# Slots of the LRU, the order of the last projections, and HGRN scores per head in a hybrid recurrent trunk

## The chip, the cores and the metric

The kernel runs on one core of one Trainium2 chip, in one launch. The metric is the time of one execution in microseconds on the device. A profiled execution gives a page and a trace; its span is the time from the first to the last instruction that the profiler saw. Engines are PE (TensorE; PEld is its weight load), DVE (VectorE), ACT (ScalarE), POOL (GpSimd) and SP, which only starts transfers.

## What is computed

One layer of a trunk with 1024 channels reads a prompt of 1024 tokens and eight single tokens of other sequences with states of their own. RMSNorm, one input projection with 3456 columns, three groups of heads that read the same input, one output projection with a residual, and an MLP of width 4096. Cut to what matters here, for HGRN2 (6 heads, 64 keys, 64 values, chunks of 64 tokens) and for the RG-LRU (256 channels):

```python
# RWKV-7, 6 heads: per token, S = S*diag(w) + (S @ -kk)(kk*a)^T + v k^T;  out = S r
# HGRN2, per head and chunk of 64 tokens, b = cumsum(log f):
dmat = exp(b[t] - b[s]) where s <= t
att[t, s] = sum_k q[t, k] * kin[s, k] * dmat[t, s, k]
o = att @ v + (q * exp(b)) @ S
S = exp(b_last)[:, None] * S + (kin * exp(b_last - b)).T @ v
# RG-LRU: xb, gate = split(pl);  h[t] = a[t] h[t-1] + u[t];  out = h * gelu(gate)
```

Everything is float32. Dense projections are done as three products of rounded halves: each operand is split into a high part (wh, xh) and the rest (wl, xl), and wh·xh, wh·xl and wl·xh are added.

## The kernel before

The prompt is cut into two halves of 512 tokens (the second carries the eight single tokens as well). RWKV and HGRN each have three pairs of heads; one pair fills the 128 partitions, a head on each 64. A step such as h1 is pair 1 of HGRN, r2 pair 2 of RWKV, l0 the first 128 channels of the LRU, w the low-rank columns of RWKV. Names end in the pair and the half: in2944_1_0 is the projection's columns from 2944 (l0's first) in half 1.

**Order on PE.** PE's row is written in program order; the other engines' order is made by a scheduler. The function weave (L106) merges seven recurrent streams and a filler. The streams are the inverses of RWKV (products W and Y, L624), its chains over chunks (ch, L703), its finish (L758), HGRN with the single tokens (L928 to L1115) and the LRU (L1148); two of them are inverses. The filler is projections() (L1334), which yields dense products: the input projection in the order of the table ORDER, then the output projection (out0 to out7) and the first part of the MLP. weave keeps a clock of its own, now; each stream yields a due time (D1 to D42, from a table) or an event to wait for, and whenever no stream is due, a filler row is taken. Where the filler can't go on, the small products of the streams stand in PE's row by themselves.

**Slots.** The outputs of a projection stay in tiles until their recurrence has run. take("hpm") (L398) makes the filler wait until one of eight slots is free. A pair of HGRN takes four (th, q, iv, gs), a tile of the LRU three: xb, gl and gq, the square of gl that the tanh form of GeLU needs. hg_run and lru give them back at their ends.

**Weights.** load_w (L283) loads 512 KB through SP into raw and rounds it to wh on ACT (L291). For names in SOON, DVE subtracts to get wl (L293); for the others ACT writes −wh and a transfer on POOL's queue adds the weights to it (L295, L296). There are two buffers each of wh and wl.

**HGRN's scores.** The exponent of b[t] − b[s] is not bounded as a product of two factors over a whole chunk, so the scores are built on six levels. On level l, blocks of 2·2^l tokens are halved; scaled (L964) makes, with b relative to the block's middle, keys kq for the earlier half and queries rq for the later half, and gram (L984) multiplies them. In gram the eight chunks are eight fp32 matmuls. The lhsT is a chunk of kq on 128 rows (two heads of 64 keys, 64 tokens), the rhs a chunk of rq with 64 columns: 32 later tokens for head 0 and 32 for head 1. That both heads can share the rows, rq is padded: for head 0's columns the rows of head 1 are zero and the other way round. Two such tiles, rqs, are zeroed once and used by turns, and DVE writes the two non-zero quarters in two operations (L981). The result, 128 × 256 in one PSUM bank, is put into att under a mask by one copy_predicated (L992). PSUM tag h has two banks, so the next level can run while the copy of this one is still to come. A level is run six times for three pairs and two halves, 36 in all. An fp32 matmul is recorded as two instructions on PE: a gram of eight is x16 in the profile.

The other names: ho are HGRN's outputs, hoT their transposes, hsq and hso the head norms and sample outputs, oT and gate the finish of RWKV, gs and hs values of roots on POOL (L152), lg the gates of the LRU.

Of the kernel before, what the change touches and what calls it, by code (L numbers as in the profile page):

```python
# [9 lines left out]
F32 = mybir.dt.float32  # L10
F32R = mybir.dt.float32r
I32 = mybir.dt.int32
AF = mybir.ActivationFunctionType
ALU = mybir.AluOpType
# [3 lines left out]
P = 128  # L18
# [7 lines left out]
HT = 512  # L26
HW = HT + NB
QT = 256
NQ = QT // 64
C = 64  # L30
NCK = HT // C
# [9 lines left out]
SOON = tuple(f"in{col}_0" for col in (1152, 1280, 0, 384, 768, 2944, 3200, 1408, 1792, 2176, 2560)) + \  # L41
    ("out0_0", "out1_0") + tuple(f"out{m}_1" for m in range(8)) + tuple(f"w1_{f}" for f in range(4))
PRI = [-100, 0, 0, 300, 300, 300, 100, 300]
ORDER = [[(x[0], int(x[1])) for x in half.split()] for half in ("r0 w0 l0 h0 r1 l1 h1 r2 h2", "w0 r0 h0 r1 h1 r2 h2 l0 l1")]
NFB = FF // (FB * P)

COL_R, COL_K, COL_V, COL_WA, COL_G = 0, 384, 768, 1152, 1280
# [1 line left out]
COL_LX, COL_LG = 2944, 3200  # L49
# [3 lines left out]
def kernel(ctx: ExitStack, tc: tile.TileContext, i, o):  # L53
    nc = tc.nc
    V, S, G, PE = nc.vector, nc.scalar, nc.gpsimd, nc.tensor
    act = S.activation
# [7 lines left out]
    def ps(tag, name):  # L64
        return psum.tile([P, 512], F32, tag=tag, name=name, bufs=PS_BUFS[tag])
# [6 lines left out]
    def mm(out, lhsT, rhs, start=True, stop=True):  # L72
        n, m = rhs.free_size(), lhsT.free_size()
        reshape(lhsT.shape[0], m)
        now[0] += n / 2200 if rhs.dtype == F32R else max(n, 112) / 580 if m > 64 else max(n, 36) / 1000
        PE.matmul(out, lhsT, rhs, start=start, stop=stop)  # L76
# [67 lines left out]
    def bc(ap, shape):  # L144
        return ap.to_broadcast(shape)
# [32 lines left out]
    id64, smask, lmask = cmask[:, 0, :], cmask[:, 1:3, :], cmask[:, 3:9, :]  # L178
# [217 lines left out]
    free = {"pm": RPM, "hpm": HPM}  # L396
# [30 lines left out]
    def take_out(hf, out, pt):  # L427

        if hf == 0:
            V.tensor_tensor(out, pt, rb0, op=ALU.mult)  # L430
        else:
            S.copy(out, pt)
# [518 lines left out]
    def hg_half(j, hf, lf, kin, q, iv, gs):  # L951
# [8 lines left out]

        att = pool.tile([P, 2, NCK // 2, C], F32, tag="att", name=f"att_{n}", bufs=1)
        A4 = [P, 2, NCK // 2, C]

        def scaled(l):  # L964

            hh = 1 << l
            kq = pool.tile([P, HW], F32, tag="kq", name=f"kq{l}_{n}", bufs=2)[:, 0:HT]
            rq = rqs[l % 2]
            pat = "p (m r j) -> p m r j"
            b4 = bf.rearrange(pat, r=2, j=hh)  # L970
            k4 = kq.rearrange(pat, r=2, j=hh)
            nblk = HT // (2 * hh)
            V.tensor_tensor(k4, b4, bc(b4[:, :, 0:1, hh - 1:hh], [P, nblk, 2, hh]), op=ALU.subtract)
            act(k4[:, :, 0, :], k4[:, :, 0, :], AF.Exp, scale=-1.0)
            act(k4[:, :, 1, :], k4[:, :, 1, :], AF.Exp)
            kin4 = kin[:, 0:HT].rearrange(pat, r=2, j=hh)
            q4 = q[:, 0:HT].rearrange(pat, r=2, j=hh)
            G.tensor_tensor(k4[:, :, 0, :], k4[:, :, 0, :], kin4[:, :, 0, :], op=ALU.mult)
            for h in range(2):
                hp = slice(h * 64, h * 64 + 64)  # L980
                V.tensor_tensor(rq[hp, h, :].rearrange("p (m j) -> p m j", j=hh), k4[hp, :, 1, :], q4[hp, :, 1, :], op=ALU.mult)  # L981
            return kq, rq

        def gram(l, kq, rq):  # L984

            hh = 1 << l
            pt = ps("h", f"gram{l}_{n}")[:, 0:4 * C]
            pt4 = pt.rearrange("p (h c t) -> p h c t", h=2, t=C // 2)
            for c in range(NCK):
                op_ = slice((c % 2) * 64, (c % 2) * 64 + 64)  # L990
                mm(pt4[op_, :, c // 2, :], kq[:, c * C:(c + 1) * C], rq[:, :, c * C // 2:(c + 1) * C // 2])
            V.copy_predicated(att.rearrange("p h c (m r j) -> p (h c) m r j", r=2, j=hh)[:, :, :, 1, :],  # L992
                              bc(lmask[:, l, :].rearrange("p (m r j) -> p m r j", r=2, j=hh)[:, None, :, 1, :].bitcast(I32),
                                 [P, NCK, C // (2 * hh), hh]),
                              pt.rearrange("p (x m j) -> p x m j", x=NCK, j=hh))


        vt_ = pool.tile([P, 4, P], F32, tag="vt", name=f"vt_{n}", bufs=1)
# [130 lines left out]
    def lru_proj(t, hf):  # L1129
        if hf == 1:  # L1130
            yield ("LRU", t, 0)
        x = []
        for w in ("xb", "gl", "gq"):
            yield from take("hpm")
            x.append(hp_tile(f"l{w}{t}_{hf}"))
        xb, gl, gq = x
        G.tensor_copy(xb[:, 0:3], lcar[:, t, 0:3])
        yield from in_proj(hf, COL_LX + t * P, lambda pt, c0, n: take_out(hf, xb[:, 3 + c0:3 + c0 + n], pt))

        def evac_g(pt, c0, n):  # L1140
            take_out(hf, gl[:, c0:c0 + n], pt)
            act(gq[:, c0:c0 + n], gl[:, c0:c0 + n], AF.Square)

        yield from in_proj(hf, COL_LG + t * P, evac_g)
        lruin[t, hf] = x
        ev(("lru", t, hf), 1.5)

    def lru(t, hf):  # L1148
        yield ("lru", t, hf)
        xb, gl, gq = lruin[t, hf]  # L1150
        n = HT if hf == 0 else HW
        s0 = hf * HT

        def f(ap):
            return ap[:, 0:n]


        V.tensor_scalar(f(gq), f(gq), 0.044715, 1.0, op0=ALU.mult, op1=ALU.add)
        V.tensor_tensor(f(gq), f(gq), f(gl), op=ALU.mult)
        act(f(gq), f(gq), AF.Tanh, scale=math.sqrt(2.0 / math.pi))  # L1160
        V.scalar_tensor_tensor(f(gl), f(gq), 1.0, f(gl), op0=ALU.add, op1=ALU.mult)

        def cw(j):
            return vec("cw", 2 * j + t)

        xc = hgp.tile([P, HW], F32, tag="xc", name=f"lxc{t}_{hf}", bufs=1)
        V.tensor_scalar(f(xc), xb[:, 3:3 + n], cw(3), vec("cb", t), op0=ALU.mult, op1=ALU.add)
        cv = cst[:, t, 0:24].rearrange("p (b j) -> p b j", j=3)
        for j in range(3):
            V.scalar_tensor_tensor(xc[:, 0:HT], xb[:, j:j + HT], cw(j), xc[:, 0:HT], op0=ALU.mult, op1=ALU.add)  # L1170
            if hf == 1:
                V.scalar_tensor_tensor(xc[:, HT:HW], cv[:, :, j], cw(j), xc[:, HT:HW], op0=ALU.mult, op1=ALU.add)
        if hf == 0:
            V.tensor_copy(lcar[:, t, 0:3], xb[:, HT:HT + 3])
        else:

            so = small.tile([P, 36], F32, tag="lso", name=f"lso{t}", bufs=1)
            V.tensor_copy(so[:, 9:12], xb[:, HT:HT + 3])
            sv = so[:, 12:36].rearrange("p (b j) -> p b j", j=3)
            V.tensor_copy(sv[:, :, 0:2], cv[:, :, 1:3])  # L1180
            V.tensor_copy(sv[:, :, 2], xb[:, 3 + HT:3 + HW])
        rt, it = xb, gq
        yield D39
        for g, (dst, bias) in enumerate(((rt, hba), (it, hbx))):
            for c0, w in (((0, 512),) if hf == 0 else ((0, 260), (260, 260))):
                pt = yield from bank_o(f"lg{t}_{g}_{hf}_{c0}")
                mm(pt[:, 0:w], lruw[:, 2 * g + t, :], xc[:, c0:c0 + w])
                used_o()
                act(dst[:, c0:c0 + w], pt[:, 0:w], AF.Tanh, bias=bias[:, t:t + 1], scale=0.5)
                yield D40  # L1190

        V.scalar_tensor_tensor(f(xc), f(it), 1.0, f(xc), op0=ALU.add, op1=ALU.mult)
        m = gq
        act(f(m), f(rt), AF.Exp, bias=nsp2[:, t:t + 1], scale=nsp2[:, t:t + 1])
        act(f(rt), f(rt), AF.Tanh, bias=sp2[:, t:t + 1], scale=sp2[:, t:t + 1])
        V.scalar_tensor_tensor(f(m), f(m), 1.0, f(rt), op0=ALU.add, op1=ALU.mult)
        V.tensor_scalar(f(rt), f(m), -1.0, 1.0, op0=ALU.mult, op1=ALU.add)

        V.scalar_tensor_tensor(f(m), f(rt), 1.0, f(m), op0=ALU.add, op1=ALU.mult)
        V.tensor_scalar(f(m), f(m), 1e-12, None, op0=ALU.max)  # L1200
        act(f(m), f(m), AF.Sqrt)
        V.scalar_tensor_tensor(f(m), f(m), 0.5, f(xc), op0=ALU.mult, op1=ALU.mult)
        hs = xc
        V.tensor_tensor_scan(hs[:, 0:HT], rt[:, 0:HT], m[:, 0:HT], 0.0 if hf == 0 else lcar[:, t, 3:4], op0=ALU.mult, op1=ALU.add)
        if hf == 1:
            V.tensor_tensor(hs[:, HT:HW], rt[:, HT:HW], cst[:, t, 24:32], op=ALU.mult)
            V.tensor_tensor(hs[:, HT:HW], hs[:, HT:HW], m[:, HT:HW], op=ALU.add)
        V.scalar_tensor_tensor(mix[6 + t][:, s0:s0 + n], f(gl), 0.5, f(hs), op0=ALU.mult, op1=ALU.mult)
        free["hpm"] += 3
        ev(("LRU", t, hf), 14.0)  # L1210
        if hf == 0:
            V.tensor_copy(lcar[:, t, 3:4], hs[:, HT - 1:HT])
            return
        V.tensor_copy(so[:, 0:9], hs[:, HT - 1:HW])
        nc.gpsimd.dma_start(o["lru"][t], so)
# [390 lines left out]
```

## Time and profile before

| what | us |
| --- | --- |
| median of three runs | 1594.58 |
| the three runs | 1597.8, 1592.06, 1594.58 |
| the profiled execution | 1598.09 |
| its span | 1596.3 |
| the scores on PE, 576 records, busy | 24.7 |
| the projection's three products on PE, busy | 222.2, 220.6, 221.7 |
| the square of gl on ACT, six operations, busy | 2.8 |

A row of the profile's groups or of the timeline names line, engine, operation and tile, with shapes as partitions by elements (for a matmul the lhsT as rows by columns, then the output), the number of instructions after x, and times. In the timeline the first number is the start within the span and the second how long it took, both in us; in brackets stands how long the engine had stood idle before it, and what it waited for. In the groups, busy us and mean ns of one come first, then the idle time before. In the waits view the numbers are us in total, how many, and the longest. In the windows view each engine has its busy time in the stretch and the number of its instructions; PEclk is the clock that TensorE was granted, as a share of full speed. Matmuls follow each other in a pipeline, so a row's own length runs into the next; the distance between starts is what a row costs.

### The profile page before, as it was taken

What the parts mean: (1) busy time and instruction counts of PE and PEld (TensorE: products, weight loads), DVE (VectorE), ACT (ScalarE), POOL (GpSimd) and SP (SyncE); (2) the same over time, 40 slices, a digit from 0 to 9 for tenths busy, and PEclk for the clock granted to TensorE, in tenths of its full rate; (3) what the DMA queues carried; (4) which work ended last, traced back from release to release, by engine and by line L of the source; (5) the groups of instructions that cost most, each with busy time, mean ns of one, the idle gap of its engine ahead of it and who ended that gap; (6) DMA issues with size and microseconds to landing.
All of it is one profiled execution on the core that took longest, in us unless ns stands there. A gap on an engine that the chain in (4) does not pass through costs nothing.

```text
span 1596.3 us, 30293 instructions
## 1 busy us (share of the span) xinstructions
PE 1501.6 (94%) x12536; PEld 1323.8 (83%) x12536; DVE 770.7 (48%) x1799; ACT 664.2 (42%) x1435; POOL 382.8 (24%) x531
## 2 busy tenths in 40 slices
PE   8879998998998989888899999999999999999997
PEld 6767776898997888777698989998989998989887
DVE  7778756766466657764465322222222222322224
ACT  4544656546346454454344423233232423233132
POOL 4553224225235245232222010101111010111011
PEclk9999999999899999978899999999999999999999
DMA  4325334334233344204533453535454454544242
GB/s 160 115 68 107 80 76 93 72 81 112 61 82 90 71 103 100 55 29 114 139 110 103 106 92 82 106 80 106 80 106 80 99 100 90 96 88 98 53 94 107
DMA packets 53081, 146.89 MB, mean 92 GB/s; under 512 B 6960, under 2 KB 7248, under 8 KB 52944
## 3 DMA queue, kind: packets, MB, share of 16 engines
q0 software_dynamic: 22976, 65.33, 24.7%
q1 hardware_dynamic: 29824, 79.61, 15.5%
q8 instruction: 98, 1.61, 0.4%
q14 instruction: 39, 0.32, 0.1%
q10 hardware_dynamic: 144, 0.04, 0.0%
HBM read 138.87 MB, written 6.07 MB: 91 GB/s over the span
## 4 chain that ended last, share of the span: by engine, by line
PE 45%; issue 5%; DMA 4%; DVE 3%; ACT 2%; POOL 1%; POOLq 0%; ACTq 0%; DVEq 0%
PE up L76 21%; PE dn L76 20%; PE out L76 2%; DMA raw_out<-in_w_out 1%; DMA wl_out<-in_w_out 1%; DMA wl_w<-in_w 1%; DMA raw_w<-in_w 1%; PE ch L76 1%; ACT wh_out L291 1%; PE in L76 1%; DVE wl_out L293 0%; PE fin L81 0%; DMA w<-in_w 0%; DVE ml L1244 0%; ACT wh_w L291 0%
## 5 line engine op out<-in xcount | busy, mean ns | idle before, releaser
L76 PE MATMUL in<-xl,wh_in 128*128 128x512 f32 (+3 forms) x648 | 222.2, 343 | 1.9 <-DVE xl L385 1.9
L76 PE MATMUL in<-xh,wl_in 128*128 128x512 f32 (+3 forms) x648 | 220.6, 340 | 3.4 <-DMA wl_in<-in_w_in 1.9
L76 PE MATMUL dn<-hh,wl_w 128*128 128x264 f32 (+2 forms) x696 | 222.9, 320 | 0.7 <-DMA wl_w<-in_w 0.6
L76 PE MATMUL dn<-hh,wh_w 128*128 128x264 f32 (+2 forms) x696 | 223.0, 320 | 0.0
L76 PE MATMUL dn<-hl,wh_w 128*128 128x264 f32 (+2 forms) x696 | 222.9, 320 | 0.0
L76 PE MATMUL in<-xh,wh_in 128*128 128x512 f32 (+3 forms) x648 | 221.7, 342 | 0.0
L1494 DVE TENSOR_TENSOR mix<-mix,dn 128x512 f32<-128x512 f32 (+2 forms) x192 | 98.3, 512 | 242.6 <-PE dn L76 242.6
L296 POOL DMA_DIRECT2D wl_w<-in_w x86 | 75.0, 875 | 574.4 <-ACT hh L1424 301.2
L291 ACT ACTIVATE wh_w<-raw_w 128x512 fp32r<-128x512 f32 (+1 forms) x90 | 70.6, 785 | 281.0 <-PE dn L76 228.2
L1423 DVE SCALAR_TENSOR_TENSOR rl<-up,rl 128x512 f32<-128x512 f32 (+2 forms) x96 | 49.5, 516 | 202.2 <-ACT rl L1422 202.2
L76 PE MATMUL up<-nxh,wh_w 128*128 128x264 f32 (+1 forms) x512 | 144.9, 283 | 0.1
L76 PE MATMUL up<-nxl,wh_w 128*128 128x264 f32 (+1 forms) x512 | 144.2, 282 | 0.5 <-POOL nxl L1320 0.5
L76 PE MATMUL up<-nxh,wl_w 128*128 128x264 f32 (+1 forms) x512 | 144.5, 282 | 0.0
L76 PEld LDWEIGHTS dn<-hh,wl_w 128*128 128x128 f32 x696 | 130.9, 188 | 13.6 <-DMA wl_w<-in_w 3.6
L76 PEld LDWEIGHTS dn<-hl,wh_w 128*128 128x128 f32 x696 | 131.0, 188 | 10.1
L76 PEld LDWEIGHTS dn<-hh,wh_w 128*128 128x128 f32 x696 | 131.1, 188 | 9.5
L76 PEld LDWEIGHTS in<-xl,wh_in 128*128 128x128 f32 x648 | 126.5, 195 | 14.6 <-DVE xl L385 4.6
L76 PEld LDWEIGHTS in<-xh,wl_in 128*128 128x128 f32 x648 | 126.3, 195 | 14.1 <-DMA wl_in<-in_w_in 2.4
L76 PEld LDWEIGHTS in<-xh,wh_in 128*128 128x128 f32 x648 | 126.3, 195 | 9.6 <-issue 0.2
L76 PE MATMUL up<-nh,wh_w 128*128 128x512 f32 x256 | 101.6, 397 | 0.0
L76 PE MATMUL up<-nl,wh_w 128*128 128x512 f32 x256 | 101.6, 397 | 0.0
L76 PE MATMUL up<-nh,wl_w 128*128 128x512 f32 x256 | 101.5, 397 | 0.0
(461 smaller groups left out, 3283.6 us busy)
## 6 DMA issues: line engine op xcount, KB each, us to landing
raw_in<-in_w_in SPq DMA_DIRECT2D x53, 512.0 KB, 3.3
wl_in<-in_w_in POOLq DMA_DIRECT2D x43, 512.0 KB, 5.5
raw_w<-in_w SPq DMA_DIRECT2D x32, 512.0 KB, 3.3
raw_w<-in_w SPq DMA_DIRECT2D x64, 256.0 KB, 2.6
wl_w<-in_w POOLq DMA_DIRECT2D x58, 256.0 KB, 4.1
wl_w<-in_w POOLq DMA_DIRECT2D x28, 512.0 KB, 5.5
raw_out<-in_w_out SPq DMA_DIRECT2D x16, 512.0 KB, 3.4
out_y_prompt<-yt SPq DMA_DIRECT2D x16, 256.0 KB, 2.0
```

Source lines behind the costliest of these rows:

```text
L76: PE.matmul(out, lhsT, rhs, start=start, stop=stop)
L291: act(wh[:, ks], raw[:, ks], AF.Copy)
L296: G.dma_start(wl[:, ks], src[:, ks], accum_op=ALU.add)
L1423: V.scalar_tensor_tensor(rl[:, :n], pt[:, :n], 0.0, rl[:, :n], op0=ALU.max, op1=ALU.mult)
L1494: V.tensor_tensor(x2[m][:, c0:c0 + n], x2[m][:, c0:c0 + n], pt[:, :n], op=ALU.add)
```

## The change

There are three edits.

The order of the second half's projections becomes w0 r0 h0 r1 **r2 h1 h2** l0 l1 in place of w0 r0 h0 r1 **h1 r2 h2** l0 l1.

The LRU takes two slots. gq is no longer made when the gate's columns come out of PSUM, in two parts, but in lru itself, in one operation over all columns, into a tile of its own with a single buffer.

HGRN's scores are computed per head. The queries are one tile rql without padding: 256 columns, both heads on their own rows, in two halves used by turns, written by one DVE operation a level; the padded tiles rqs stay for the queries of ho. gram does sixteen matmuls: for each chunk and head one with 64 rows, 64 columns of kq and 32 of rq. Each head writes a bank of its own, so a level takes both banks of tag h, and each head has a masked copy of half the size.

```diff
-ORDER = [... ("r0 w0 l0 h0 r1 l1 h1 r2 h2", "w0 r0 h0 r1 h1 r2 h2 l0 l1")]
+ORDER = [... ("r0 w0 l0 h0 r1 l1 h1 r2 h2", "w0 r0 h0 r1 r2 h1 h2 l0 l1")]
...
+        rql = pool.tile([P, 2, HT // 2], F32, tag="kt", name=f"rql_{n}", bufs=1)
...
-            rq = rqs[l % 2]
+            rq = rql[:, l % 2]
...
+            V.tensor_tensor(rq.rearrange("p (m j) -> p m j", j=hh), k4[:, :, 1, :], q4[:, :, 1, :], op=ALU.mult)
+            return kq, rq
+
+        def gram(l, kq, rq):
+
+            hh = 1 << l
+
+            pts = [ps("h", f"gram{l}_{h}_{n}")[:, 0:2 * C] for h in range(2)]
+            for c in range(NCK):
+                for h, hp in enumerate(brow):
+                    mm(pts[h][(c % 2) * 64:(c % 2) * 64 + 64, c // 2 * (C // 2):(c // 2 + 1) * (C // 2)], kq[hp, c * C:(c + 1) * C], rq[hp, c * C // 2:(c + 1) * C // 2])
             for h in range(2):
-                hp = slice(h * 64, h * 64 + 64)
-                V.tensor_tensor(rq[hp, h, :].rearrange("p (m j) -> p m j", j=hh), k4[hp, :, 1, :], q4[hp, :, 1, :], op=ALU.mult)
-            return kq, rq
-
-        def gram(l, kq, rq):
-
-            hh = 1 << l
-            pt = ps("h", f"gram{l}_{n}")[:, 0:4 * C]
-            pt4 = pt.rearrange("p (h c t) -> p h c t", h=2, t=C // 2)
-            for c in range(NCK):
-                op_ = slice((c % 2) * 64, (c % 2) * 64 + 64)
-                mm(pt4[op_, :, c // 2, :], kq[:, c * C:(c + 1) * C], rq[:, :, c * C // 2:(c + 1) * C // 2])
-            V.copy_predicated(att.rearrange("p h c (m r j) -> p (h c) m r j", r=2, j=hh)[:, :, :, 1, :],
...
+                V.copy_predicated(att[:, h].rearrange("p c (m r j) -> p c m r j", r=2, j=hh)[:, :, :, 1, :],
...
-        for w in ("xb", "gl", "gq"):
+        for w in ("xb", "gl"):
...
-            take_out(hf, gl[:, c0:c0 + n], pt)
-            act(gq[:, c0:c0 + n], gl[:, c0:c0 + n], AF.Square)
...
+        gq = hgp.tile([P, HW], F32, tag="lq", name=f"lq{t}_{hf}", bufs=1)
...
+        act(f(gq), f(gl), AF.Square)
...
-        free["hpm"] += 3
+        free["hpm"] += 2
```

The order of instructions moves with it. First PE, at the place where before the projection of l0 (in3200 is its second half) ends and that of l1 can't start; W, Y and ch are the inverse and the chain of RWKV's pair 2, half 1, gram the scores of h2 in half 1, lg the gates of l0. Before:

```order
L76 MATMUL in3200_1_256_8092<-xh7_3192,wl_in3200_1_7686 128x264
L76 MATMUL gram4_2_1_8186<-rq0_196,kq4_2_1_8126 64x2x32 x8
L76 MATMUL W3_2_1_1_8213<-xm_2_1_1_7880,sa_2_1_1_7878 64x64 x8
L76 MATMUL ch_2_1_0_8079<-st0_2_1_0_8167,az_186 128x64
L76 MATMUL Y3_2_1_1_8226<-ym_2_1_1_7879,wm3_2_1_1_8212 64x64 x8
L76 MATMUL ch_2_1_0_8079<-rh1_2_1_0_8224,yz_187 128x64
L76 MATMUL gram5_2_1_8239<-rq1_197,kq5_2_1_8179 64x2x32 x8
L76 MATMUL ch_2_1_0_8079<-mv_2_1_0_7418,bt_2_1_0_7214 128x64
L76 MATMUL W4_2_1_1_8256<-xm_2_1_1_7880,sa_2_1_1_7878 64x64 x8
L76 MATMUL Y4_2_1_1_8278<-ym_2_1_1_7879,wm4_2_1_1_8255 64x64 x8
L76 MATMUL lg0_0_1_0_8289<-lxc0_1_8200,lruw_204 128x260
```

Now the same W3 to W5 stand ahead of l0's projection, between the last dense row of h1 and h2 (columns 2816) and in2944, beside the end of h1: hoT, hso and hsq; ahead of these rows, behind the last dense one, stand W2, ho of h1 with its 32 matmuls, and Y2, with 26 ch rows between and behind them.

```order
L81 MATMUL hoT_1_1_8096<-ident_79,hot_1_1_8012 128x128 x4
L76 MATMUL Y3_2_1_1_8102<-ym_2_1_1_7736,wm3_2_1_1_8066 64x64 x8
L76 MATMUL ch_2_1_0_8118<-st2_1_184,az_186 128x64
L76 MATMUL W4_2_1_1_8129<-xm_2_1_1_7737,sa_2_1_1_7735 64x64 x8
L76 MATMUL hsrow1_8139<-hsdg1_8122,bones_84 128x512
L76 MATMUL ch_2_1_0_8118<-rh0_2_1_0_8126,yz_187 128x64
L76 MATMUL Y4_2_1_1_8146<-ym_2_1_1_7736,wm4_2_1_1_8128 64x64 x8
L81 MATMUL oT_1_1_1_8157<-ident_79,ot_1_1_1_8077 128x128 x4
L76 MATMUL ch_2_1_0_8118<-mv_2_1_0_7011,bt_2_1_0_6811 128x64
L76 MATMUL gate_1_1_1_8170<-pm_xg1_3608,gup_162 128x256
L76 MATMUL hso1_8173<-hq1_1_6529,hsst1_8120 64x1 x16
L76 MATMUL W5_2_1_1_8194<-xm_2_1_1_7737,sa_2_1_1_7735 32x32 x8
```

So the place without dense rows has moved from behind l0's projection to ahead of it, and the end of h1 stands in it.

Next POOL's queue, between two weight loads of the output projection; st2_1 is RWKV's state, lso1 the LRU's, xr the residual's input. Before:

```order
L296 DMA wl_out4_0_8884<-in_w_out 128x1024
L756 DMA out_p_wkv<-st2_1_184 128x64
L1262 DMA xr4_0_8992<-in_xt 128x512
L1262 DMA xr4_0_8992<-in_xt 128x512
L152 TENSOR_TENSOR gs_2_1_1_8952<-gs_2_1_1_8952,mhalf_64 128x4
L1215 DMA out_lru<-lso1_8733 128x36
L296 DMA wl_out5_0_8987<-in_w_out 128x1024
```

And now:

```order
L296 DMA wl_out4_0_9080<-in_w_out 128x1024
L1098 TENSOR_TENSOR hsdg2_9339<-cmask_88,hi2_1_7574 128x512
L152 TENSOR_TENSOR gs_2_1_1_9143<-gs_2_1_1_9143,mhalf_64 128x4
L1213 DMA out_lru<-lso1_8858 128x36
L943 DMA out_p_hgrn<-hst7_2_1_9203 128x64
L1096 DMA hsst2_9337<-in_hgrn 128x512
L152 TENSOR_TENSOR hs_2_1_9247<-hs_2_1_9247,mhalf_64 128x8
L1260 DMA xr4_0_9277<-in_xt 128x512
L1099 TENSOR_TENSOR hsst2_9337<-hsst2_9337,hfs2_8488 128x512
L296 DMA wl_out5_0_9272<-in_w_out 128x1024
```

The end of pair 2 of HGRN (its state, and what the single tokens need) now stands between the two loads. On DVE, each level of the scores has two masked copies and one product of the queries where it had one and two; an early level of pair 0, half 0 before, with its keys, and then now:

```order
L973 TENSOR_TENSOR kq4_0_0_1335<-b_0_0_1032 128x512
L992 COPY_PREDICATED att_0_0_1035<-cmask_88,gram2_0_0_1293 128x64x4
L981 TENSOR_TENSOR rq0_196<-kq4_0_0_1335,hq0_0_701 64x256 x2
L693 COPY_PREDICATED ym_0_0_1_1160<-cmask_88,Y1_0_0_1_1314 128x64x2
L728 COPY mv_0_0_0_812<-ch_0_0_0_1307 128x64
```
```order
L992 COPY_PREDICATED att_0_0_1035<-cmask_88,gram1_0_0_0_1213 128x64x2
L974 TENSOR_TENSOR kq3_0_0_1304<-b_0_0_1032 128x512
L992 COPY_PREDICATED att_0_0_1035<-cmask_88,gram1_1_0_0_1214 128x64x2
L980 TENSOR_TENSOR rql_0_0_1036<-kq3_0_0_1304,hq0_0_701 128x256
L430 TENSOR_TENSOR praw_k1_0_1114<-in512_0_0_1123,mix5_74 128x512
```

The keys of a later level stand between the two copies.

More of the change, by code (lines that the diff above doesn't have):

```diff
@@ L43 @@
 PRI = [-100, 0, 0, 300, 300, 300, 100, 300]
-ORDER = [[(x[0], int(x[1])) for x in half.split()] for half in ("r0 w0 l0 h0 r1 l1 h1 r2 h2", "w0 r0 h0 r1 h1 r2 h2 l0 l1")]
+ORDER = [[(x[0], int(x[1])) for x in half.split()] for half in ("r0 w0 l0 h0 r1 l1 h1 r2 h2", "w0 r0 h0 r1 r2 h1 h2 l0 l1")]
 NFB = FF // (FB * P)
@@ L978, in scaled @@
             G.tensor_tensor(k4[:, :, 0, :], k4[:, :, 0, :], kin4[:, :, 0, :], op=ALU.mult)
-            for h in range(2):
-                hp = slice(h * 64, h * 64 + 64)
-                V.tensor_tensor(rq[hp, h, :].rearrange("p (m j) -> p m j", j=hh), k4[hp, :, 1, :], q4[hp, :, 1, :], op=ALU.mult)
+            V.tensor_tensor(rq.rearrange("p (m j) -> p m j", j=hh), k4[:, :, 1, :], q4[:, :, 1, :], op=ALU.mult)
             return kq, rq
@@ L986, in gram @@
             hh = 1 << l
-            pt = ps("h", f"gram{l}_{n}")[:, 0:4 * C]
-            pt4 = pt.rearrange("p (h c t) -> p h c t", h=2, t=C // 2)
+            pts = [ps("h", f"gram{l}_{h}_{n}")[:, 0:2 * C] for h in range(2)]
             for c in range(NCK):
-                op_ = slice((c % 2) * 64, (c % 2) * 64 + 64)
-                mm(pt4[op_, :, c // 2, :], kq[:, c * C:(c + 1) * C], rq[:, :, c * C // 2:(c + 1) * C // 2])
[L992 to L995, printed above, removed]
+                for h, hp in enumerate(brow):
+                    mm(pts[h][(c % 2) * 64:(c % 2) * 64 + 64, c // 2 * (C // 2):(c // 2 + 1) * (C // 2)], kq[hp, c * C:(c + 1) * C], rq[hp, c * C // 2:(c + 1) * C // 2])
+            for h in range(2):
+                V.copy_predicated(att[:, h].rearrange("p c (m r j) -> p c m r j", r=2, j=hh)[:, :, :, 1, :],
+                                  bc(lmask[:, l, :].rearrange("p (m r j) -> p m r j", r=2, j=hh)[:, None, :, 1, :].bitcast(I32),
+                                     [P, NCK // 2, C // (2 * hh), hh]),
+                                  pts[h].rearrange("p (x m j) -> p x m j", x=NCK // 2, j=hh))
         vt_ = pool.tile([P, 4, P], F32, tag="vt", name=f"vt_{n}", bufs=1)
@@ L1132, in lru_proj @@
         x = []
-        for w in ("xb", "gl", "gq"):
+        for w in ("xb", "gl"):
             yield from take("hpm")
             x.append(hp_tile(f"l{w}{t}_{hf}"))
-        xb, gl, gq = x
+        xb, gl = x
         G.tensor_copy(xb[:, 0:3], lcar[:, t, 0:3])
         yield from in_proj(hf, COL_LX + t * P, lambda pt, c0, n: take_out(hf, xb[:, 3 + c0:3 + c0 + n], pt))
-        def evac_g(pt, c0, n):
-            take_out(hf, gl[:, c0:c0 + n], pt)
-            act(gq[:, c0:c0 + n], gl[:, c0:c0 + n], AF.Square)
-        yield from in_proj(hf, COL_LG + t * P, evac_g)
+        yield from in_proj(hf, COL_LG + t * P, lambda pt, c0, n: take_out(hf, gl[:, c0:c0 + n], pt))
         lruin[t, hf] = x
@@ L1149, in lru @@
         yield ("lru", t, hf)
-        xb, gl, gq = lruin[t, hf]
+        xb, gl = lruin[t, hf]
+        gq = hgp.tile([P, HW], F32, tag="lq", name=f"lq{t}_{hf}", bufs=1)
         n = HT if hf == 0 else HW
```

## Prediction

> **What bounds the kernel now.** I read the page first, for the engine that sets the end.
>
> ```profile
> span 1596.3 us, 30293 instructions
> PE 1501.6 (94%) x12536; PEld 1323.8 (83%) x12536; DVE 770.7 (48%) x1799; ACT 664.2 (42%) x1435; POOL 382.8 (24%) x531
> PE   8879998998998989888899999999999999999997
> PEclk9999999999899999978899999999999999999999
> ```
>
> PE is busy for 94% of the span, so the kernel ends when PE has worked through its hand-planned row. The time can only change in three ways: less work for PE, less time in which PE stands still, or less time at a low clock. Standing still and low clock both lie in the first half; the slices with 7 and 8 in PEclk say where. Next, therefore, the windows view, cut at the stages of the plan: up to 302 us the first half of the sequence, to 468 us the part whose order the change leaves nearly as it was, to 788 us the rest of the recurrences and the output projection's start, then the MLP.
>
> ```profile
> core 0: us, PE busy (x) PEld busy (x) DVE busy (x) ACT busy (x) POOL busy (x), PEclk, DMA share, GB/s
> 0.00:302.00 302.00, 270.79 (x2344) 214.98 (x2345) 216.29 (x490) 159.92 (x341) 114.36 (x180) 0.98 0.39 98
> 302.00:468.00 166.00, 157.37 (x1959) 145.27 (x1958) 103.93 (x291) 83.62 (x222) 50.15 (x73) 0.94 0.37 81
> 468.00:662.00 194.00, 178.10 (x2320) 160.95 (x2319) 127.98 (x373) 100.39 (x276) 80.77 (x110) 0.99 0.38 86
> 662.00:691.00 29.00, 25.83 (x349) 21.62 (x348) 17.27 (x48) 12.04 (x29) 6.60 (x12) 0.71 0.17 38
> 691.00:715.00 24.00, 20.71 (x197) 19.28 (x197) 15.62 (x38) 15.18 (x51) 8.06 (x9) 0.86 0.12 36
> 715.00:737.00 22.00, 16.97 (x65) 13.21 (x65) 10.37 (x26) 6.04 (x9) 5.24 (x7) 0.77 0.29 76
> 737.00:788.00 51.00, 42.42 (x213) 33.48 (x213) 22.48 (x44) 25.26 (x47) 11.59 (x17) 0.93 0.63 159
> 788.00:1596.00 808.00, 789.43 (x5102) 715.04 (x5100) 256.80 (x495) 261.81 (x468) 106.03 (x125) 1.00 0.44 93
> ```
>
> I count as lost in a stretch its idle time plus the share of the clock that was missing: length less PE busy, plus (1 − PEclk) times PE busy. That gives 17.7 us for 468 to 662 (9% of it), then 10.7, 6.2, 8.9 and 11.6 us for the four stretches to 788: 37.4 us of 126, or 30%. From 468 to 788 us it is 55 us, and 265 us is work at full clock. This is what the new order can touch. The reason stands in the timeline of PE. At 662 us the dense projection runs out, because the next one, l1's, needs three slots and one is free, and the chained small products of RWKV and HGRN stand alone:
>
> ```profile
> 668.89 0.69 PE L76 MATMUL gram<-rq,kq 128*64 128x64 f32 x16
> ...
> 671.48 0.68 PE L76 MATMUL Y<-ym,wm 64*64 64x64 f32 x16 [0.79 <-ACT wm L672]
> ...
> 672.45 0.69 PE L76 MATMUL gram<-rq,kq 128*64 128x64 f32 x16
> ...
> 675.01 1.12 PE L76 MATMUL W<-xm,sa 64*64 64x64 f32 x16 [1.09 <-DVE xm L697]
> 676.59 1.12 PE L76 MATMUL Y<-ym,wm 64*64 64x64 f32 x16 [0.46 <-ACT wm L672]
> ```
>
> The product Y of sixteen records takes 0.68 us at 671 and 1.12 us at 677: the clock has fallen, and over the stretch to 691 it is 0.71 in the windows. The waits view of PE for 468 to 788 us names what ends its idle time there:
>
> ```profile
> PE out L76 <- DMA wl_out<-in_w_out: 8.1, 4, 4.4
> PE gate L76 <- DVE mix L782: 4.7, 3, 2.9
> PE hoT L81 <- DVE hot L1083: 3.7, 2, 2.2
> PE ch L76 <- DVE st L737: 3.6, 6, 1.2
> PE hsq L76 <- DVE hssq L1115: 2.8, 2, 2.2
> PE ch L76 <- DVE mv L728: 2.5, 2, 2.3
> ```
>
> A third of it is weights not yet landed, the rest results of DVE that a chain needs next.
>
> **The change part by part.** *Slots and order.* With two slots for an LRU tile, h2 (four) and l0 (two) leave two of eight, so l1's projection starts without waiting for the end of h2: the stop at 662 is gone. But h1 and h2 now follow each other and hold all eight, so l0's projection must wait for h1's run to end. The order shows what stands there: from W2 of pair 2 over the tail of h1 (ho, hoT, hso, hsq) to in2944 there is no dense row. Of its work ho is the dearest:
>
> ```profile
> 588.51 2.03 PE L76 MATMUL ho<-vt,att 64*64 64x64 f32 x32
> 590.47 1.72 PE L76 MATMUL ho<-hst,rq 128*64 128x64 f32 x32
> ...
> 603.35 0.66 PE L81 MATMUL hoT<-ident,hot 128*128 128x128 f32 x4 [2.23 <-DVE hot L1083]
> ```
>
> I add its work up at full clock. ho is 3.7 us (588.51 to 592.19). Three W, three Y and W5 at the 0.6 that separates such products from the next row are 4.2. A record of gram takes 0.61/16 = 0.038 (rows below); 29 ch products of two such are 2.2. Transposes, hsrow, gate, hso and hsq I put at 1.4. That is 11.5, say 12 us, an estimate. Its length is set by the chain: ho begins behind W2 (0.7), takes 3.7, and hoT came 11 us after its end here, with dense rows between. Only behind hoT stand Y3, W4, Y4 and W5. By the rows above W to Y took 1.6 us (675.01 to 676.59) and Y to the next W 3.5 (671.48 to 675.01) without filler, so Y3 to W5 is 3.5 + 1.6 + 3.5 = 8.6. The sum is 24 us, and 12 of it are lost, standing still or at a low clock. That is the loss of 662 to 691 (10.7) over again, at another place. What goes for good is the stretches behind it: the chains that ran at 691 to 737 beside little else now run beside l0, l1 and the first output weights, all dense.
>
> So, for the work of 265 us after 468: 12 in the bare stretch lose 12. The other 253 run with filler, as 468 to 662 did, which lost 17.7 on 176.3 of work, 10%: 25. The weights of the output projection lost 8.1 before and I keep 8. Sum 45, against 55: **10 us less**. The bounds: with the bare chain wholly hidden it would be 22 less; with the losses of 715 to 737 (8.9) and some of the 6.2 of 691 to 715 back, nothing.
>
> *Weights.* Why 8 stays: the largest wait has a cause that the queue of POOL shows.
>
> ```profile
> 757.99 1.48 POOL L152 TENSOR_TENSOR gs<-gs,mhalf 128x4 f32<-128x4 f32 x1 [6.28 <-DVE gs L770]
> 759.44 0.61 POOL L1215 DMA_DIRECT2D out_lru<-lso  x1
> 760.05 0.96 POOL L296 DMA_DIRECT2D wl_out<-in_w_out  x1
> ```
> ```profile
> 765.53 0.73 PE L76 MATMUL out<-mh,wl_out 128*128 128x512 f32 x1 [4.39 <-DMA wl_out<-in_w_out]
> ```
>
> The load of wl_out5 stood behind a root that waited 6.28 us for DVE, was issued at 760.05 and landed 5.5 us later. In the new order more stands between wl_out4 and wl_out5: eight operations for four, the states of HGRN among them. Those waits stay, and tiles in3072 and in3328 get some like them.
>
> *The scores.* PE has 16 passes a level where it had 8, each on half the rows and half the columns. An fp32 pass is counted twice, so 32 records for 16. What one level takes now is read from its start to the next row's:
>
> ```profile
> 234.41 0.69 PE L76 MATMUL gram<-rq,kq 128*64 128x64 f32 x16
> 235.02 0.32 PE L76 MATMUL ch<-mv,bt 128*128 128x64 f32 x1
> ```
> ```profile
> 158.41 0.69 PE L76 MATMUL hS<-vt,kt 64*64 64x64 f32 x32
> 159.04 0.50 PE L76 MATMUL in<-xh,wl_in 128*128 128x512 f32 x1
> ```
> ```profile
> 394.49 1.10 PE L76 MATMUL rso<-sm_r,s_st 64*64 64x1 f32 x32 [2.09 <-DVE s_st L860]
> 395.52 0.32 PE L76 MATMUL ch<-rh,yz 128*128 128x64 f32 x1
> ```
>
> Now 0.61 us. hS has the new form: 32 records of 64 rows, going round all four quarters of the array, 0.63 us. rso, whose 32 keep to two quarters, took 1.03 although each has one column. So between 0.63 and 1.03; I take 0.63, as the new scores too go round four quarters and two banks: 36 levels by 0.02, **0.7 us more**, at most 15. A rule speaks against this edit. The Trainium skill, "TensorE: Matmul & The Clock Gate", section "Wait — 56ns, not 53.3ns?", says that start-to-start never drops below about 25 ns, however small N. By it alone 32 passes would need 0.80 us, an estimate, and the levels 7 us more; hS, at 20 ns a record, disagrees.
>
> On DVE:
>
> ```profile
> L981 DVE TENSOR_TENSOR rq<-kq,hq 64x256 f32<-64x256 f32 x72 | 38.5, 535 | 5.5 <-ACT kq L975 3.6 <-ACT hq L432 0.8 <-PE ho L76 0.2
> L992 DVE COPY_PREDICATED att<-cmask,gram 128x256 f32<-128x256 int32 x36 | 19.3, 535 | 0.2
> L693 DVE COPY_PREDICATED ym<-cmask,Y 128x128 f32<-128x128 int32 x48 | 15.9, 331 | 15.3 <-PE Y L76 15.0
> ```
>
> Half of the 72 products go: 36 by 0.535, 19.3 us. Each masked copy becomes two of half the size, which cost 0.331 in the row of Y: 72 by 0.331 less 19.3, 4.5 us more. DVE does 14.7 us less of the 514 it does up to 788, about 3%. The waits on DVE in the list sum to 17.3 us; 3% of these is 0.5, and as the operations that go stand in HGRN's own chain, I take **1 us less**. What the two copies add is a wait: both banks of tag h are taken at each level, so the next level's passes stand until the second copy is through. With that, W, Y and ch queued behind them on PE would wait; the next level came 3.6 us later in the row (668.89 to 672.45), and the copies are 0.7 us, so I cost it at nothing; without that cover it would be the second copy's 0.33 at 36 levels, 12 us.
>
> *The square of the gate* goes from the evacuation into the run of LRU, the same columns on ACT once in place of twice; ACT is at 42% and waits for PE or DVE, so nothing. It stands in the chain of l0 and l1, which has the MLP behind it as slack. The zeroing of two tiles stays.
>
> **Sum:** −10 + 0.7 − 1 = −10.3. The profiled execution took 1598.1 us (1.8 outside the span), 3.5 above the median of the three runs, 1594.6; on it this gives 1587.8, and on the median 1584.3, say 1584.
>
> **The rivals.** *The losses only move* (chance 0.2). The bare stretch is new, and the waits of 715 to 737 on mix, hssq and mv, which are chains of DVE and not of slots, come back at the chains' new ends. Then 8.9 of the 10 are not saved, or all: 1593 to 1596. For it speaks that the order puts h1's, pair 1's and pair 2's ends close together; against it, that dense rows follow at once for 250 us.
>
> *Weights late behind POOL* (0.14, slower). In the new order more of HGRN's and LRU's work lies in the output projection, and POOL issues weight loads in program order: in3072, in3328 and out2 to out7 each stand behind a root, a state's store or a gate that waits for DVE, at wl_out5 above all. If each of these eight waits 3.5 us (the largest is 4.4), that is 28 in place of 8, +20: about 1604. It cancels the gain from 2.3 us a tile (18.3 in place of 8) and gives a measurable loss from 2.9. For it: the fence of POOL; against it: the other three waits on wl_out sum to 3.7.
>
> *The scores serial* (0.04). If the 64-row passes of a head don't overlap the other's, a level takes rso's 1.03: 36 by 0.41, +15, near 1598. hS speaks against it. The floor of 25 ns on that page of the Trainium skill is a milder form of this and would give about 1590.
>
> *A full gain* (0.06): hoT comes early and the bare chain is filled: 22 less, 1572.
>
> **How the numbers follow.** The forecast has what is left, 0.56, with its own range from 1574 to 1590. The range of all cases: down to 1567, the full gain with half of the weights' waits gone; up to 1602, which takes in the moved losses and the serial case, and leaves out most of the late weights. About 0.3%, 5 us, is what a measurement of this kernel can tell from no change: faster is below 1589.8, slower above 1599.4. Faster: 0.53 of the forecast, 0.06 of the full gain, 0.01 of the moved losses: 0.60. Slower: 0.12 of the late weights, 0.02 of the serial scores, 0.02 of the moved losses: 0.16. The same: 0.24.
>
> **What would show it.** Right: no fall of the clock at the place of l1's projection, one new stretch without dense rows ahead of in2944, 20 to 26 us long, with the clock at about 0.7; a loss of some 45 us between 468 us and the MLP; scores at 0.63 us a level; DVE 15 us less busy. Wrong: waits on wl_in and wl_out of over 16 us together, a level of the scores over 0.8 us, waits of gram on DVE's copies, or a loss of 50 and more with the waits on mix and hssq as they were.

## The result and the profile after

The changed kernel takes 1580.05 us (median of four runs, 1576.89 to 1583.56), the kernel before 1594.14 us beside it (four runs). The ratio is 0.9904, with a 95% interval from 0.9883 to 0.9926: 14 to 15 us less. The profiled execution took 1583.56 us, with a span of 1581.8 us against 1596.3.

The page of the changed kernel, its first lines and the row of the clock in slices:

```profile
span 1581.8 us, 31488 instructions
PE 1500.9 (95%) x13112; PEld 1322.7 (84%) x13112; DVE 757.3 (48%) x1799; ACT 665.3 (42%) x1433; POOL 382.5 (24%) x531
PEclk9989999998999999799999999999999999999999
```

PE is busy as long as before, DVE 13.4 us less. The one deep fall of the clock has moved from about 680 us to about 640. The windows view, cut at the stages of the new order:

```profile
core 0: us, PE busy (x) PEld busy (x) DVE busy (x) ACT busy (x) POOL busy (x), PEclk, DMA share, GB/s
0.00:296.60 296.60, 273.58 (x2537) 217.90 (x2537) 211.75 (x489) 161.38 (x341) 115.03 (x179) 0.96 0.40 100
296.60:456.00 159.40, 151.55 (x2149) 140.31 (x2148) 98.95 (x292) 83.59 (x220) 50.32 (x74) 0.97 0.39 84
456.00:613.50 157.50, 147.88 (x1969) 134.78 (x1967) 99.75 (x295) 83.75 (x219) 57.19 (x83) 0.98 0.35 79
613.50:651.00 37.50, 33.13 (x459) 28.95 (x459) 17.22 (x55) 12.82 (x53) 17.92 (x23) 0.75 0.34 81
651.00:704.00 53.00, 49.12 (x516) 42.36 (x514) 37.24 (x94) 30.04 (x66) 14.78 (x22) 0.98 0.32 77
704.00:722.00 18.00, 11.73 (x77) 9.45 (x78) 10.46 (x29) 7.21 (x11) 3.41 (x6) 0.81 0.49 115
722.00:770.60 48.60, 41.39 (x318) 31.93 (x317) 25.04 (x54) 24.33 (x60) 17.56 (x21) 0.96 0.59 143
770.60:1581.80 811.20, 792.52 (x5101) 717.02 (x5099) 256.93 (x495) 262.17 (x468) 106.29 (x125) 0.99 0.44 93
```

The first two rows end at the places where those of before ended (302 and 468 us), the seventh where 788 stood. So 12 us had been gained at 456 us, ahead of everything that the new order moves; 5.4 us came between there and the output projection's second half (314.6 for 320); and the last stage took about 3 us longer. Idle time plus missing clock, worked out as in the prediction, is 12.6, 12.7, 4.9, 8.5 and 8.9 us in the five rows from 456 on: 47.5 us for 55. Since 7.5 us less are lost there and the stretch is only 5.4 us shorter, some 2 us of work at full clock have come in besides.

The new stretch without dense rows is there. PE's timeline from W2 to l0's first rows (of the rows left out, most are ch):

```profile
620.61 0.68 PE L76 MATMUL W<-xm,sa 64*64 64x64 f32 x16
...
621.59 1.15 PE L76 MATMUL ho<-vt,att 64*64 64x64 f32 x32
622.66 1.20 PE L76 MATMUL ho<-hst,rq 128*64 128x64 f32 x32
623.79 0.43 PE L76 MATMUL ch<-rh,yz 128*128 128x64 f32 x2
...
629.54 0.63 PE L81 MATMUL hoT<-ident,hot 128*128 128x128 f32 x4 [1.65 <-DVE gs L765]
630.10 0.68 PE L76 MATMUL Y<-ym,wm 64*64 64x64 f32 x16
...
632.58 1.12 PE L76 MATMUL W<-xm,sa 64*64 64x64 f32 x16 [1.43 <-DVE rh L724]
...
642.21 0.64 PE L76 MATMUL W<-xm,sa 32*32 32x32 f32 x16
...
643.23 0.56 PE L76 MATMUL in<-xh,wh_in 128*128 128x256 f32 x1
```

It is 22.6 us long, and from 632 us on the products take the length of a halved clock. A second new loss stands at 704 to 722 us, where PE waits for the input lxc of l1's gates. First PE's row, then DVE's queue ahead of it (mix is l0's last result, lxc here l1's first one):

```profile
711.21 1.23 PE L76 MATMUL lg<-lxc,lruw 128*128 128x260 f32 x2 [5.96 <-DVE lxc L1168]
```
```profile
705.74 0.70 DVE L1206 SCALAR_TENSOR_TENSOR mix<-lgl,lxc 128x520 f32<-128x520 f32 x1
...
706.90 0.55 DVE L1165 TENSOR_SCALAR lxc<-lxb,vt 128x520 f32<-128x520 f32 x1
```

The LRU's two tiles run behind each other on the one buffer of lxc; l1's work starts when l0's ends, and PE's row has its product 5.96 us too early. In the waits of PE from 456 to 771 us this is now the largest, and the weights have become small:

```profile
PE lg L76 <- DVE lxc L1168: 6.0, 1, 6.0
PE ch L76 <- DVE st L737: 3.6, 6, 1.1
PE out L76 <- DMA wl_out<-in_w_out: 3.1, 2, 2.0
PE gate L76 <- DVE mix L782: 2.5, 3, 1.0
PE hsq L76 <- DVE hssq L1115: 2.1, 1, 2.1
```

The scores, on PE from their start to the next row, beside two different neighbours:

```profile
232.84 0.67 PE L76 MATMUL gram<-rql,kq 64*64 64x32 f32 x32
233.33 0.67 PE L76 MATMUL W<-xm,sa 64*64 64x64 f32 x16
...
237.95 0.67 PE L76 MATMUL gram<-rql,kq 64*64 64x32 f32 x32
238.55 0.43 PE L76 MATMUL ch<-st,az 128*128 128x64 f32 x2
```

Ahead of ch a level takes 0.60 us for 0.61 before, ahead of W, which has the same shape of array, 0.49. On DVE the groups of the scores are (the copies of Y are as before):

```profile
L980 DVE TENSOR_TENSOR rql<-kq,hq 128x256 f32<-128x256 f32 x36 | 22.1, 619 | 7.3 <-ACT kq L976 7.3
L992 DVE COPY_PREDICATED att<-cmask,gram 128x128 f32<-128x128 int32 x72 | 23.6, 341 | 10.8 <-PE gram L76 10.6
```

The queries' product went from 38.5 to 22.1 us, and the masked copies from 19.3 to 23.6.

### The profile page after: what moved, and what is told of

Read it like the earlier page. It is cut to its first block, busy times and chain, and to the rows that moved or that the text cites. A ratio compares the mean times of both kernels' runs of the same rounds, so it can differ in the third digit from the quotient of the medians.

```text
span 1581.8 us, 31488 instructions
## 1 busy us (share of the span) xinstructions
PE 1500.9 (95%) x13112; PEld 1322.7 (84%) x13112; DVE 757.3 (48%) x1799; ACT 665.3 (42%) x1433; POOL 382.5 (24%) x531
## 4 chain that ended last, share of the span: by engine, by line
PE 72%; DVE 10%; issue 6%; ACT 5%; DMA 4%; POOL 2%; POOLq 0%; SPq 0%; DVEq 0%; ACTq 0%
PE up L76 22%; PE dn L76 19%; PE in L76 13%; PE out L76 4%; PE ch L76 2%; PE W L76 2%; PE Y L76 2%; PE sc L76 1%; PE gram L76 1%; DMA wl_out<-in_w_out 1%; DVE rq L1035 1%; PE ho L76 1%; DMA raw_in<-in_w_in 1%; DMA wl_w<-in_w 1%; ACT gsq L768 1%
## 5 line engine op out<-in xcount | busy, mean ns | idle before, releaser
L76 PEld LDWEIGHTS in<-xl,wh_in 128*128 128x128 f32 x648 | 127.4, 197 | 13.4 <-DVE xl L385 4.2
L1420 ACT ACTIVATE rl<-up 128x512 f32<-128x512 f32 (+2 forms) x96 | 43.3, 451 | 141.0 <-PE up L76 140.9
```

The source lines that it names most:

```text
L1420: act(rl[:, :n], pt[:, :n], AF.Relu)
```

## The experiments

My theory was that of the prediction (A): the order and the slots carry the gain, as one edit, and the scores next to nothing. The rivals, formed on the profile after: the scores have the larger part (C), or the early gain is scatter (D), or the order does it by itself (B). First each edit alone, and two of them together. The order is the table's line, the slots are the LRU's lines, the scores those of rql and gram:

```diff
-"w0 r0 h0 r1 h1 r2 h2 l0 l1"
+"w0 r0 h0 r1 r2 h1 h2 l0 l1"
...
-        for w in ("xb", "gl", "gq"):
+        for w in ("xb", "gl"):
...
-            rq = rqs[l % 2]
+            rq = rql[:, l % 2]
```

The order alone.

> Only the table of the projections' order is changed; the LRU keeps three slots and the scores stay as they were. Theory A (the order and the slots belong together, and the gain behind 468 us is theirs): h1 and h2 hold all eight slots, then l0 takes three of the four that h1 gives back, and l1 needs three where one is free, so a second place without dense rows stays as it was before. At most 3 us are gained or lost: 1591 to 1598. Rival B (the order by itself breaks up the row of chains, the slots are by the way): 1585 to 1588.

Measured 1592.09 us, 0.9977 (0.9959 to 0.9994). As A has it. In the windows from 466.9 us on both stops stand one after the other, ahead of l0 (first row) and ahead of l1 (second row):

```profile
620.10:659.20 39.10, 34.19 (x459) 29.96 (x458) 18.77 (x59) 11.95 (x51) 17.51 (x23) 0.72 0.29 74
...
668.20:695.90 27.70, 22.68 (x205) 18.45 (x203) 17.33 (x50) 13.20 (x40) 7.86 (x12) 0.69 0.29 65
```

The slots alone.

> Only the LRU's two slots; old order, old scores. Theory A: l1 no longer waits for the end of h2, so the stretch of 662 to 691 us with 10.7 us lost becomes shorter, but in the old order l0 and l1 then run earlier and the chains of pair 2 and h2 end beside the output projection; 4 to 8 us less, 1586 to 1590. Rival B: nothing by itself, 1592 to 1597, since the filler that l1 supplies there is missing later.

Measured 1573.84 us, 0.9868 (0.9847 to 0.9889). More than either theory gave, and 6 us ahead of the whole change: something in the change costs.

The scores alone.

> Only the scores per head on 64 rows; old order, three slots. My prediction: the scores cost PE 0.7 us more and relieve DVE for 1, so within 2 us of before, 1592 to 1597. Rival C, from the profile of the changed kernel, in which 11.5 of 14.5 us are already gained at 456 us, ahead of all rows that the order moves: the scores are the larger part, 7 to 11 us less, 1583 to 1588, as waits of W, Y, ch and pb on DVE get shorter. Rival D: those 11.5 us are the scatter of single executions (the profiled one of before is its slowest but one): then this is at 1594 as by the prediction, with some 5 us from one run to the next.

Measured 1586.73 us, 0.9937 (0.9916 to 0.9959). Rival C's number, not mine, and not scatter.

Order and slots.

> Order and two slots together, with the old scores. My prediction gives these two edits 10 of the 10.3 us: 1582 to 1587. Rival C (the scores have the larger part): 1588 to 1592, 3 to 6 us less, as the stretch behind 456 us gained 6.5 in the profile and the MLP gave 3.6 back.

Measured 1584.16 us, 0.9923 (0.9904 to 0.9942). My number for the pair (−10, measured −11 to −12), but against the slots alone (0.9868) the order costs 9 us. The pair was right as a sum, but it hides a larger gain and a loss.

Next the two other pairs, and what the scores gain by. For the latter the planner's clock is set after a level to what the old scores would have added, so that PE's row is that of before but for the scores:

```diff
+            told = now[0] + (0.12 if shape[0] != (P, 64) else 0) + NCK * 0.064
             for c in range(NCK):
...
+            now[0], shape[0] = told, (P, 64)
```

> The scores alone, and the planner's clock is advanced as by the old scores, so that PE's row is that of before but for the scores' own rows; what is left is what the engines do. If the scores' gain comes from DVE (one write less a level, shorter masked copies), this is as fast as the scores alone, within 3 us. If it comes from the planner placing other rows, this is at 1592 to 1597, as before.

Measured 1590.47 us, 0.9979 (0.9961 to 0.9996): between the two cases. By the medians about a third of the 10 us that the scores bring alone is the engines' work (by the interval, between 1 and 6 us); the rest came with the row that the planner then makes.

The queries in two writes, on top of the old plan.

> As the run with the old plan, but the queries of each level are written in two DVE operations on 64 rows, as before, still without padding: DVE then does 4 us more than before in place of 12 to 13 less, and PE's row is the same. If the relief of DVE is what the scores gain by, this loses all of it and is at 1594 to 1600. If PE's passes on 64 rows gain by themselves (no change of the array's shape between W, Y and the scores), it stays within 2 us of the run with one write.

The edit:

```diff
-            V.tensor_tensor(rq.rearrange("p (m j) -> p m j", j=hh), k4[:, :, 1, :], q4[:, :, 1, :], op=ALU.mult)
+            for hp in brow:
+                V.tensor_tensor(rq[hp].rearrange("p (m j) -> p m j", j=hh), k4[hp, :, 1, :], q4[hp, :, 1, :], op=ALU.mult)
```

Measured 1592.5 us, 0.9992 (0.9977 to 1.0008). The gain can't be told from none, but the interval overlaps that of one write, so whether DVE's relief or PE's passes bring the 3 us is not settled.

All but the order.

> All but the order. If the order has a part of its own beside the slots, this is 3 to 6 us slower than the changed kernel: 1583 to 1586. If the order matters little once an LRU tile takes two slots, it is within 2 us of 1580.

Measured 1572.01 us, 0.9866 (0.9843 to 0.9889). Neither number: the order doesn't help, it costs 6 us here.

All but the slots.

> All but the two slots. If the slots are needed for the order to pay (l1 has to wait for the end of h2 otherwise), this is 5 to 10 us slower than the changed kernel, 1585 to 1590; if not, within 2 us of 1580.

Measured 1589.47 us, 0.9976 (0.9958 to 0.9994). As expected: without the slots the order doesn't pay. Alone it brought 3 to 4 us, and beside the scores it loses 6 by the medians (0.9937 without it).

The last four ask for causes. If the slots pay by removing the stop, the stop put back must take the gain away, without undoing the LRU's edit. One slot fewer in the second half does that:

```diff
         for hf in range(2):
+            free["hpm"] -= hf
             for group, j in ORDER[hf]:
```

> As all but the order, but in the second half one of the eight slots is withheld, so that l1 has to wait for the end of h2 again: 143 small products stand without a dense row between l0's and l1's projections, as 127 did before; nothing else of the change is undone. If the stop is what the slots save, this loses most of their 14 to 21 us: 1584 to 1592. If the slots gain by something else (the square in one operation, its own tile), it stays within 3 us of 1572.

Measured 1586.94 us, 0.9954 (0.9933 to 0.9975), against 0.9866 with eight: 14 us lost to one slot. The stretch in which l1 waits, in the windows of this run:

```profile
652.60:681.40 28.80, 25.47 (x395) 21.73 (x393) 14.83 (x43) 11.12 (x24) 5.84 (x12) 0.70 0.18 38
```

It is the row of 662 to 691 us of before over again (29.00 us, clock 0.71). The control, the LRU as in the change but holding a third slot, in the kernel before:

```diff
+        yield from take("hpm")
...
-        free["hpm"] += 2
+        free["hpm"] += 3
```

> Order and scores of before, and the LRU as in the change (two tiles, the square in lru in one operation, a tile of its own), but a third slot is taken and held without a use, so that every wait for slots is that of before. If the slots are all that counts, this is as before, 1592 to 1597; if the square's move gains by itself, below 1590.

Measured 1590.14 us, 0.9977 (0.9959 to 0.9995). Between the cases: the square's move and its tile bring some 4 us of the 21, by the interval at most 7; the waits for slots are the rest, by subtraction. Its profiled execution took only 1580.84 us. PE's row in it is that of before, and the stop stands there, but the clock doesn't fall:

```profile
658.00:687.00 29.00, 24.73 (x381) 21.29 (x379) 21.27 (x56) 16.75 (x47) 9.10 (x14) 1.00 0.19 48
```

Between two dense rows stand 16.2 us in it (664.94 to 681.11), 22.1 in the kernel before (668.68 to 690.77). So the same stop costs less when the clock doesn't fall. Whether that is this execution's luck or the kernel's isn't known, as one execution of each kernel is profiled.

If the order's price is the stretch ahead of l0, an order that keeps r1 and r2 in a row but has l0 ahead of h2 must not pay it:

```diff
-w0 r0 h0 r1 r2 h1 h2 l0 l1
+w0 r0 h0 r1 r2 h1 l0 h2 l1
```

> The last pairs of RWKV in a row as in the change, but l0 ahead of h2: the order is w0 r0 h0 r1 r2 h1 l0 h2 l1. The row of PE then has no stretch of more than 70 small products without a dense one, where the changed kernel has 152 ahead of l0. If this stretch is the price of the order, 1570 to 1575; if r1 and r2 in a row cost by themselves (two inverses and chains beside each other, HGRN late), 1577 to 1582 as the changed kernel.

Measured 1562.16 us (five runs, 1559.47 to 1565.1), 0.9798 (0.9774 to 0.9823). That is 17 us ahead of the changed kernel and the fastest of all. So r1 and r2 in a row need not cost anything. The 17 us are not the stretch's alone: PE's wait of 6.0 us for l1's lxc is gone too (it was 6.8 with order and slots; here the longest wait of the gates is 1.1), and no run takes the one away without the other. The windows from the same place to the MLP's first row, of before, of the change, of the slots alone, of this run and of all but the order, each with the length first:

```profile
467.70:844.30 376.60, 335.69 (x3545) 299.00 (x3544) 226.33 (x579) 179.36 (x441) 122.70 (x165) 0.94 0.37 91
```
```profile
456.10:826.20 370.10, 334.56 (x3736) 297.47 (x3736) 222.19 (x579) 178.22 (x439) 121.30 (x165) 0.94 0.38 92
```
```profile
462.50:814.50 352.00, 324.04 (x3545) 291.79 (x3544) 224.74 (x579) 179.20 (x439) 123.57 (x165) 0.98 0.37 97
```
```profile
456.20:808.40 352.20, 325.77 (x3737) 293.39 (x3736) 219.60 (x579) 177.30 (x439) 121.25 (x165) 0.97 0.38 97
```
```profile
454.30:817.60 363.30, 330.27 (x3735) 297.17 (x3735) 219.38 (x579) 179.00 (x439) 123.75 (x165) 0.95 0.37 94
```

In the third and the fourth, which have no stretch of more than 10 us without dense rows, the clock is 0.97 to 0.98 for 0.94, and 18 to 25 us are gone. The run with l0 ahead of h2 keeps besides what the scores gain before 456 us. All but the order, the fifth, loses 11 us to the slots alone here. In the row that the planner makes with the new scores and the old order no dense product stands from 570.64 to 582.79 us; PE waits there for HGRN's state:

```profile
575.04 0.45 PE L76 MATMUL ho<-hst,rq 128*64 128x64 f32 x4 [2.16 <-DVE hst L1060]
```

With the slots alone the same piece is 9.0 us long, and the scores alone and the run with seven slots have it at 12.4 and 12.3 us. This piece is not the whole of the 11 us. So the 11 us by which l0 ahead of h2 is faster than all but the order are not shown to be the gain of r1 and r2 in a row; behind 456 us it is no faster than the slots alone.

Last, the slots and the scores with the row of the slots alone, to see whether the scores' gain adds up there.

> Two slots and the scores per head, old order, and the planner told the old cost of the scores, so that PE's row is that of the run with the slots alone but for the scores. If the engines gain by the scores what they gained by them in the old kernel with the old plan (4 us), this is 1568 to 1571, ahead of the run with the slots alone (1573.8) and of all but the order (1572.0). If the scores have nothing left to give once no stretch is bare, 1572 to 1575.

Measured 1575.38 us, 0.9884 (0.986 to 0.9909). The second case: beside the slots, in the old order, the scores give nothing that can be told from zero.

## Why the prediction was right, and where its steps were not

The time was forecast at 1584 us and is 1580; −10.3 of some −14. The sum held, in part by luck: the slots' gain was put too low and the order's price was not seen, and the two cancel.

**The stop at 662 and the new stretch.** Both came as said. The stop was the slots', shown by holding one slot back (+14 us). The new stretch was put at 24 us with 12 lost; it is 22.6 us long, and the window of 613.5 to 651 us around it lost 12.7. That the 12 came out is luck, since only 8.8 of them lie in the stretch itself (4.4 idle, and the clock of the row below); the other 3.9 are dense rows behind it, which ran at a clock of 0.50 and for which the prediction has no term.

```profile
620.61:643.23 22.62, 18.25 (x298) 15.12 (x297) 11.56 (x36) 9.35 (x45) 11.50 (x17) 0.76 0.31 76
```

The parts of that 24 were wrong: I read ho as 3.7 us "at full clock" from rows at a clock of 0.59 (588.51 to 592.19); it takes 2.2 (621.59 to 623.79). hoT came 5.8 us behind it in place of 11, and Y3 to W5 took 12.1 in place of 8.6. What I didn't see is whose price it is. I costed order and slots as one edit, so the loss of the order (9 us beside the slots, 6 beside slots and scores) stayed inside a gain (21 us for the slots alone). The step that failed is the first sentence on the order: that l0 waits for h1 was set down as what comes with the slots, and it was not asked whether the slots need the new order at all. In the old order, with two slots, nothing waits there.

**The rest with filler**, 10% of the work: 456 to 613.5 lost 12.6 on 144.9 of work, 9%. But 704 to 722 lost 8.5 around the wait for l1's gates, of which the prediction has nothing: it gave the chain of l0 and l1 slack up to the MLP, but PE's row has the gates' products among those of the output projection, and PE waits at them. It takes the place of the waits of 691 to 737, so the first rival was partly right. The wait is there with order and slots (6.8 us) and in the change (6.0), and in no run without both of these edits, nor in the one with l0 ahead of h2. How the order's price divides between it and the new stretch stays open.

**The weights** were kept at 8 and are 3.1 us in two waits, although more stands ahead of wl_out5 on POOL. The slower rival, late weights, fell. That PE comes to those tiles with other rows in between may be why; it was not tried by itself.

**The scores on PE**: 0.63 us a level was forecast, 0.60 measured, and 0.49 ahead of a product of the same shape. The serial rival, 1.03, fell. The Trainium skill's floor of 25 ns from start to start ("TensorE: Matmul & The Clock Gate", section "Wait — 56ns, not 53.3ns?") doesn't hold for these passes: 32 in 0.60 us are 19 ns. The Trainium skill's page "TensorEngine Tiling (Array Packing)", section "Key Properties", says that different tiles can load and multiply in parallel, and with that the row agrees.

**The scores on DVE**: 14.7 us less was forecast, 13.4 are less. The product of the queries takes 0.619 us on 128 rows for 0.535 on 64, so 16.4 us went and not 19.3; the masked copies added 4.3. That is 12.1 of the 13.4. What this is worth was put at 1 us and is about 3 with the old plan (0.9979), 10 with the plan that the planner makes of it in the old kernel (0.9937), 3 on top of order and slots (0.9923 to 0.9904), and nothing that shows on top of the slots (0.9868 to 0.9866). This term was mis-sized, and its mechanism was incomplete: a new cost of the scores moves the planner's whole row, in the first half of the sequence too, which I had called nearly unchanged. There 12 us went in the profile. But the same place came at 462.4 to 467.7 us in the five profiled kernels with the old scores, and at 454.3 to 456.2 in the six with the new scores and their own plan, so about 9 are the scores'. With the new scores and the old plan it came at 460.1 to 463.4 in three, so by the means about 3 of the 9 are the engines' and the rest the row's. Beside the slots the gain is lost again behind 456 us, with the planner's own row in part by the piece shown above; the rest of it, and the case with the old plan, stay open.

**The square** cost nothing that shows: with a third slot held the kernel is some 4 us faster, not slower.

## What to carry to other kernels

Where a filler keeps an engine busy, count per edit the rows that stand without it: in the order of instructions 127 small products stood in one piece before and 152 after, at another place, while the slots alone left no such stretch, nor did the slots with l0 ahead of h2. A new cost in the planner can make such a stretch as well, as all but the order shows. An edit that removes a stop and one that moves the order should be priced apart, since the second can make a new stop and hide in the gain of the first. And a duration taken from a trace needs the clock of its own row beside it.

## What the runs showed of the hardware

The clock can stay low far into dense work. In the changed kernel dense rows begin again at 643.23 us, and rows of the same product (256 columns) still start 0.21 us apart at 650; at 653 us those of 264 columns start 0.12 apart:

```profile
649.14 0.41 PE L76 MATMUL in<-xh,wl_in 128*128 128x256 f32 x1
649.36 0.41 PE L76 MATMUL in<-xh,wh_in 128*128 128x256 f32 x1
...
652.76 0.28 PE L76 MATMUL in<-xh,wl_in 128*128 128x264 f32 x1
652.87 0.29 PE L76 MATMUL in<-xh,wh_in 128*128 128x264 f32 x1
```

So 9.4 us of dense rows ran at about half speed after the stretch had ended. It was 9.3 us with order and slots and with the order alone, at the same stretch. But this is no rule for every stop: with order and scores the clock was back before the dense rows, and in the kernel before the dense rows behind its stop, which begin at 690.77 us, start 0.12 apart almost at once.

```profile
690.98 0.28 PE L76 MATMUL in<-xl,wh_in 128*128 128x256 f32 x1
691.09 0.28 PE L76 MATMUL in<-xh,wl_in 128*128 128x256 f32 x1
691.21 0.28 PE L76 MATMUL in<-xh,wh_in 128*128 128x256 f32 x1
```

And in the profile with the third slot held the clock didn't fall at all (1.00, above). Where it falls, a stop costs more than its idle time. The Trainium skill's page "TensorE: Matmul & The Clock Gate", section "What's actually happening", says that the gate opens after at least one busy window of about 3.4 us; in the changed kernel, with a few small products between the dense rows, it took nearly three of these.

Passes of different products on 64 rows can overlap when one follows the other. In the changed kernel records of Y start among those of the scores:

```profile
243.19 0.24 PE L76 MATMUL gram<-rql,kq 64*64 64x32 f32 x1
243.19 0.22 PE L76 MATMUL Y<-ym,wm 64*64 64x64 f32 x1
243.20 0.24 PE L76 MATMUL gram<-rql,kq 64*64 64x32 f32 x1
```

This may be how a level ahead of W comes to 0.49 us; no run separates it from the shape of the array.
